# The output projection of block 2 by one level of Strassen's algorithm, its sums made from the merged tiles and the weights

## The chip, the cores and the metric

The kernel is one program on one core of a Trainium2 chip. The metric is the device time of one execution in microseconds (us); lower is better. TensorE is called PE, its weight loads PEld, VectorE DVE, ScalarE ACT, GpSimd POOL, and SyncE, which issues the DMAs, SP. Each engine takes its instructions in the order of its own queue; semaphores tie the queues together.

## The reference

Two transformer blocks over 1024 tokens of width 1024, all in float32. The change lies in the second block, at the line with `w_out`:

```
merged = g_a * (o_a @ w_branch_a[l]) + g_b * (o_b @ w_branch_b[l])
x = x + merged @ w_out[l]
h2 = rms_norm(x, norm2[l])
x = x + jnp.square(jax.nn.relu(h2 @ w_up[l])) @ w_down[l]
```

`merged` and `w_out` are 1024 x 1024; `w_up` is 1024 x 4096.

## The kernel before

A float32 product is made of three fast ones: each operand is split into a high part (ACT casts it, `hi`, L109; tiles `fh`, `hh`, `sh`, `wh`) and a low part (raw minus high, `lo`, L112, on DVE or POOL; tiles `fl`, `hl`, `sl`, `wl`), and PE adds high by high, high by low and low by high into one PSUM bank. An operand tile is 128 x 512.

The order of the instructions is made when the kernel is built. An event list (`e.at(dt, ...)`) holds the work of DVE, ACT, POOL and SP for a time `dt` ns after the present point of PE's estimated time; `e.need(tag)` brings forward whatever carries a tag that PE needs now. A `Stream` hands out one step of its list per `gap` ns until a goal that `ahead` sets; `Feed` is such a stream for operands: its steps load, combine (`comb`, a DVE sum, L1492) and split tiles. One `Feed`, `F`, serves the up and the down projection, which use Strassen's algorithm in Winograd's form already (seven products, in the order 1, 6, 7, 4, 2, 5, 3).

The stages around the change:

- `merge` (L1337) makes `merged` transposed, 16 tiles `gl`, from the two branches and splits each of them (ACT `sh`, DVE `sl`).
- `out2` (L1377) is the output projection as a plain product: two column halves, eight row tiles each, eight steps of k by three matmuls in a tile, 384 matmuls. Its weights come through the weight queue `W` under the names `wp`, split by ACT and POOL.
- `out2_evac` (L1402) follows a tile: the gather (DVE, L1407) adds half of the bank to the residual tile `x`; ACT squares it and sums the row (L407); for the second column half POOL makes 1 over the root mean square (`ry`: L1411, L117, L118) and DVE scales the row, two instructions `xs` (L1415); then the row is stored.
- `prep0` (L1606) turns the first four row tiles into eight operands for the up projection: for each of eight steps, k0 to k7, PE transposes four 128 x 128 pieces (L104) into a PSUM bank `tp` (two of them), ACT makes `hh` and `hr` (L1615, L1616), DVE makes `hl` (L1617). It is interleaved with the matmuls of the second column half. `prep1` does the rows 4 to 7 during `up_first`, the first seven products of the up projection, which follow.

## Time and profile before

| what | us |
|---|---|
| median of 3 runs | 1839.72 |
| lowest and highest | 1838.95, 1840.46 |
| the profiled execution, its own time | 1840.45 |
| its span, first to last instruction | 1838.6 |
| PE busy | 1801.7 (98%) |
| DVE, ACT, POOL busy | 1087.1, 949.3, 702.2 |

A busy PE is one that has matmuls in flight. The projection takes the span from 1107.85 us, its first matmul, to 1199.62 us, the first matmul of the up projection.

### The profile page before, as it was taken

What the parts mean: (1) busy time and instruction counts of PE and PEld (TensorE: products, weight loads), DVE (VectorE), ACT (ScalarE), POOL (GpSimd) and SP (SyncE); (2) the same over time, 40 slices, a digit from 0 to 9 for tenths busy, and PEclk for the clock granted to TensorE, in tenths of its full rate; (3) what the DMA queues carried; (4) which work ended last, traced back from release to release, by engine and by line L of the source; (5) the groups of instructions that cost most, each with busy time, mean ns of one, the idle gap of its engine ahead of it and who ended that gap; (6) DMA issues with size and microseconds to landing.
All of it is one profiled execution on the core that took longest, in us unless ns stands there. A gap on an engine that the chain in (4) does not pass through costs nothing.

```text
span 1838.6 us, 25740 instructions
## 1 busy us (share of the span) xinstructions
PE 1801.7 (98%) x9005; PEld 1517.9 (83%) x9005; DVE 1087.1 (59%) x2033; ACT 949.3 (52%) x1955; POOL 702.2 (38%) x684
## 2 busy tenths in 40 slices
PE   7999999999999999999999999999999998999998
PEld 6888878888898898889888888877888876888886
DVE  6578794544464656556565541467443448766775
ACT  6455553446665767556465322365555555352444
POOL 4123242512222212222111242265544456685873
PEclk9999999999999999999999999999999999999999
DMA  7101131314222221220111922514554478444522
GB/s 204 35 24 35 35 115 59 126 47 93 81 46 81 72 50 47 72 72 27 52 44 48 301 84 83 161 41 156 171 169 146 150 254 290 142 161 138 173 79 92
DMA packets 189186, 195.68 MB, mean 106 GB/s; under 512 B 16944, under 2 KB 124160, under 8 KB 189056
## 3 DMA queue, kind: packets, MB, share of 16 engines
q1 hardware_dynamic: 189056, 194.04, 33.7%
q8 instruction: 70, 1.15, 0.2%
q14 instruction: 60, 0.49, 0.1%
HBM read 141.52 MB, written 54.04 MB: 106 GB/s over the span
## 4 chain that ended last, share of the span: by engine, by line
PE 90%; DVE 3%; ACT 3%; POOL 1%; issue 1%; DMA 1%; SPq 0%; POOLq 0%; ACTq 0%; DVEq 0%
PE mm L99 40%; PE mmO L99 14%; PE mmmm L99 9%; PE mmo L99 7%; PE mmT L99 7%; PE tp L104 4%; PE S L99 4%; PE O L99 4%; DVE s L933 1%; POOL ry L118 0%; DMA wr<-in_w_up 0%; POOL fl L112 0%; DMA x<-x_d 0%; ACT junk L407 0%; PE tp L99 0%
## 5 line engine op out<-in xcount | busy, mean ns | idle before, releaser
L112 POOL TENSOR_TENSOR wl<-wr,wh 128x512 fp32r<-128x512 f32 x164 | 218.9, 1340 | 619.7 <-ACT wh L109 374.4
L99 PE MATMUL mm<-hh,wh 128*128 128x512 f32 (+1 forms) x792 | 313.4, 396 | 0.0
L99 PE MATMUL mm<-hl,wh 128*128 128x512 f32 (+1 forms) x792 | 309.7, 391 | 1.7 <-DVE hl L818 1.7
L99 PE MATMUL mm<-hh,wl 128*128 128x512 f32 (+1 forms) x792 | 309.0, 390 | 0.0
L112 POOL TENSOR_TENSOR fl<-wr,fh 128x512 fp32r<-128x512 f32 x148 | 205.6, 1402 | 129.2 <-ACT fh L109 118.3
L109 ACT CAST fh<-wr 128x512 fp32r<-128x512 f32 x192 | 115.9, 617 | 181.9 <-DVE wr L1492 135.8
L659 ACT ACTIVATE sb<-sb,nm 128x128 f32<-128x128 f32 (+2 forms) x192 | 125.6, 655 | 149.3 <-DVE nm L653 99.1
L99 PEld LDWEIGHTS mm<-hh,wl 128*128 128x128 f32 x792 | 149.4, 189 | 32.4
L99 PEld LDWEIGHTS mm<-hl,wh 128*128 128x128 f32 x792 | 149.8, 189 | 26.6 <-DVE hl L818 2.2
L99 PEld LDWEIGHTS mm<-hh,wh 128*128 128x128 f32 x792 | 149.8, 189 | 25.3
L112 DVE TENSOR_TENSOR ptl<-tp,pth 128x512 fp32r<-128x512 f32 (+2 forms) x176 | 113.4, 646 | 80.2 <-ACT pth L109 76.1
L112 POOL TENSOR_TENSOR fl<-ha,fh 128x512 fp32r<-128x512 f32 x80 | 124.5, 1574 | 47.8 <-ACT fh L109 36.3
L109 ACT CAST pth<-tp 128x512 fp32r<-128x512 f32 (+2 forms) x176 | 96.4, 548 | 74.3 <-PE tp L104 70.1
L668 DVE TENSOR_SCALAR sb<-sb,rc 128x128 f32<-128x128 f32 (+2 forms) x192 | 97.6, 508 | 6.7
L104 PE MATMUL tp<-ident,sb 128*128 128x128 f32 x648 | 99.6, 272 | 1.0 <-DVE ptl L112 0.7
L109 ACT CAST wh<-wr 128x512 fp32r<-128x512 f32 x164 | 99.2, 616 | 0.8 <-DMA wr<-in_w_in 0.4
L104 PEld LDWEIGHTS tp<-ident,sb 128*128 128x128 f32 x648 | 80.6, 140 | 22.4 <-DVE ptl L112 1.2
L99 PE MATMUL O<-pth,v 128*128 128x256 f32 (+3 forms) x264 | 93.2, 361 | 0.0
L99 PE MATMUL mmO<-hh,fh 128*128 128x512 f32 x208 | 81.6, 392 | 2.1 <-ACT pk L1758 2.1
L1492 DVE TENSOR_TENSOR wr<-wr 128x512 f32<-128x512 f32 x96 | 81.4, 848 | 3.7 <-POOL fl L112 2.4
L99 PE MATMUL S<-kh,q 128*128 128x256 f32 (+3 forms) x264 | 79.7, 315 | 2.8 <-DVE nm L653 2.8
L99 PE MATMUL mmO<-hh,fl 128*128 128x512 f32 x208 | 81.6, 393 | 0.0
(296 smaller groups left out, 4529.4 us busy)
## 6 DMA issues: line engine op xcount, KB each, us to landing
wr<-in_w_in SPq DMA_DIRECT2D x116, 256.0 KB, 3.4
ha<-hid_d SPq DMA_DIRECT2D x112, 256.0 KB, 4.2
wr<-in_w_up SPq DMA_DIRECT2D x64, 256.0 KB, 4.6
hid_d<-hc SPq DMA_DIRECT2D x64, 256.0 KB, 2.8
wr<-in_w_down SPq DMA_DIRECT2D x64, 256.0 KB, 3.8
hid_d<-pk SPq DMA_DIRECT2D x45, 256.0 KB, 3.3
wr<-in_w_out SPq DMA_DIRECT2D x32, 256.0 KB, 4.0
x_d<-x SPq DMA_DIRECT2D x32, 256.0 KB, 2.1
```

What stands on the lines that cost most here:

```text
L99: self.nc.tensor.matmul(out=out, lhsT=lhsT, rhs=rhs, start=start, stop=stop, skip_group_check=skip)
L104: self.nc.tensor.transpose(out, in_, ident)
L109: self.nc.scalar.copy(out, in_)
L112: (eng or self.nc.vector).tensor_tensor(out=out, in0=in0, in1=hi.bitcast(F32), op=ALU.subtract)
L659: ACT.activation(d[:, 0:w], d[:, 0:w], AF.Exp, bias=nm, scale=-1.0, accum_out=g.sm[:, j:j + 1])
L668: V.tensor_scalar(out=d[:, 0:w], in0=d[:, 0:w], scalar1=g.rc[:, j:j + 1], scalar2=None, op0=ALU.mult)
L933: V.tensor_tensor(out=nxt[:, a0:1040], in0=cur[:, a0:1040], in1=cur[:, a0 - n:1040 - n], op=ALU.add)
L1492: eng.tensor_tensor(out=self.raw[dst], in0=self.raw[x], in1=self.raw[y], op=op)
```

## The change

The projection becomes seven Strassen products of four 128 x 512 tiles each, with four steps of k by three matmuls: 336 matmuls. `merge` no longer splits its tiles. For q = 0 to 3 `m_sums` makes four sums of merged tiles on DVE as they become complete. A second `Feed`, `FO`, loads the 16 tiles of `w_out`, makes four combinations of them for each q (16 in all, on DVE, now L838), and splits 28 operands of each side: 56 casts on ACT, and 56 low parts, 20 of them on DVE and 36 on POOL. A product's tile is gathered on DVE (now L1554) each time its bank holds a finished sum of the products so far, 28 times; products 4, 2, 5 and 3 finish a quarter of the output, and the gather there is followed by ACT's square; 5 and 3 finish the second column half, so POOL's `ry` (L1563, L117, L118) and DVE's `xs` (L1567) follow theirs. `e.wide` gives the products three pairs of PSUM banks in turn except in products 5 and 3, when the transposes of `prep0` need a pair. The rows 6 and 7 are scaled only after `prep0` has freed the buffers. `row_steps` and `row_prod` are the functions that the down projection had, made common.

```diff
-    for ch in range(2):
-        for j in range(4):
-            W.add(f"wp{ch}{j}", [rowhalf(a["w_out_2"][0], kt, ch) for kt in (2 * j, 2 * j + 1)])
...
+    def row_steps(F, qs, more=None):
+        if more is not None:
+            for i in ORDER:
+                for q in qs:
+                    fn, *keys = more(q, i)
+                    F.source(fn, *keys)
+        def sp(q, n, i, last=True):
+            F.split((q, "a", i), (q, "a", i), True, 5)
+            F.split((q, "w", n), (q, "w", i), last, 5)
+        def cm(q, d, x, y):
+            F.comb((q, "w", d), (q, "w", x), (q, "w", y), SUB)
+        for q in qs:
+            sp(q, "11", 1, False)
+        for q in qs:
+            cm(q, "t3", "12", "22"), cm(q, "12", "12", "11"), cm(q, "11", "22", "12"), sp(q, "11", 6, False)
+        for q in qs:
+            sp(q, "t3", 7)
+        for q in qs:
+            cm(q, "11", "21", "11"), sp(q, "11", 4)
+        for i, n in ((2, "21"), (5, "12"), (3, "22")):
+            for q in qs:
+                sp(q, n, i)
+    def row_prod(F, i, qs, ahead, gather):
+        for q in qs:
+            F.s.need((q, "w", i), ahead)
+        F.flush()
+        ops = [(F.parts.pop((q, "a", i)), F.parts.pop((q, "w", i))) for q in qs]
+        go_on = i in (6, 7, 4, 3)
+        for t in range(4):
+            tc_ = slice(t * 128, t * 128 + 128)
+            if go_on:
+                e.need(("bank", t))
+            else:
+                banks[t] = e.mmt()
+            ps = banks[t]
+            for j, ((h, l), (wh, wl)) in enumerate(ops):
+                e.mm(ps, h[:, tc_], wh, j == 0 and not go_on, False, go_on)
+                e.mm(ps, h[:, tc_], wl, False, False, go_on)
+                e.mm(ps, l[:, tc_], wh, False, j == len(ops) - 1, go_on)
+                yield 650.0
+            e.at(50, lambda t=t, ps=ps: gather(i, t, ps), ("bank", t))
...
+                self.ready(src)
...
+    FO = Feed()
+    FO.look = 8
+    def wo2(q, n, j, ch):
+        r = e.u(name="wr")
+        SY.dma_start(out=r, in_=a["w_out_2"][0][(4 * j + q) * 128:(4 * j + q + 1) * 128, ch * 512:ch * 512 + 512])
+        FO.raw[q, "w", n] = r
+    MORE = {1: (("11", 0, 0),), 6: (("12", 0, 1), ("22", 1, 1)), 4: (("21", 1, 0),)}
+    def out_more(q, i):
+        ws = MORE.get(i, ())
+        return (lambda: [wo2(q, *x) for x in ws], *((q, "w", x[0]) for x in ws))
+    row_steps(FO, range(4), out_more)
+    FO.ready = lambda key: e.need(("ms", key[0])) if key[1] == "a" and key[2] > 1 else None
+    def m_sums(q):
+        m11, m12, m21, m22 = mT.pop((q, 1)), mT.pop((q + 4, 1)), mT.pop((q, 0)), mT.pop((q + 4, 0))
+        s2, s3, s4 = (e.u(name="ms") for _ in range(3))
+        V.tensor_tensor(out=s3, in0=m21, in1=m11, op=SUB)
+        V.tensor_tensor(out=m21, in0=m21, in1=m22, op=ADD)
+        V.tensor_tensor(out=s2, in0=m22, in1=s3, op=ADD)
+        V.tensor_tensor(out=s4, in0=m12, in1=s2, op=SUB)
+        for i, x in {2: m12, 3: s4, 4: m22, 5: m21, 6: s2, 7: s3}.items():
+            FO.raw[q, "a", i] = x
...
-            parts = W.get(f"ab{j}", 1 if j < 5 else 4)
+            parts = W.get(f"ab{j}", 1)
+            if j == 5:
+                for q in range(4):
+                    FO.raw[q, "a", 1] = mT[q, 1]
+                FO.load(0, 8)
+            if j > 5:
+                FO.ahead(8 * (j - 5))
...
-                mT[j, half] = split(ga, ("m", j, half), 1600.0)
+                mT[j, half] = ga
+            if j >= 4:
+                e.at(1800, lambda q=j - 4: m_sums(q), ("ms", j - 4))
...
+    held, rows_free = [], []
...
+    def out2():
+        for n, i in enumerate(ORDER):
+            if n < 4:
+                for t in range(4):
+                    x2_load(i, t)
+            if n >= 4:
+                F.load(0, n - 3)
+                F.ahead(6 * (n - 4))
+            e.wide = i not in (5, 3)
+            yield from row_prod(FO, i, range(4), 16, out2_gather)
...
+    def where(i, t):
+        return t + 4 * (GOES[i][0] == "1"), int(GOES[i][1]) - 1
+
+    def out2_gather(i, t, ps):
+        t, ch = where(i, t)
         xt = x2[t, ch]
+        V.scalar_tensor_tensor(out=xt, in0=ps, scalar=0.5, in1=xt, op0=ALU.mult, op1=ALU.add)
+        if i not in (4, 2, 5, 3):
+            return
...
-        e.at(800, lambda: sumsq(xt, ss[:, ch:ch + 1]))
+        e.at(750, lambda: sumsq(xt, ss[:, ch:ch + 1]))
...
+            if t < 6 or rows_free:
+                e.at(1650, f3, ("xs2", t))
+            else:
+                held.append((f3, ("xs2", t)))
+            xs2_t[t] = e.t + 4450
...
+        rows_free.append(True)
+        for n, (f, tag) in enumerate(held):
+            e.at(50 + 700 * n, f, tag)
...
-    run(out2(0))
-    interleave(out2(1), prep0, lambda: xs2_t.get(3), 2)
-    mT.clear()
+    interleave(out2(), prep0, lambda: xs2_t.get(3), 2)
```

Three places of the queues, with line numbers of the changed kernel where it is that.

DVE in product 1 and on into product 6 (`x2` is a residual tile in a gather, `wr` and `cb` are weight tiles and their combinations; the combination that `fh_11621` and `fl_11622`, the last operand of product 6, are split from is the last row):

```order
L1554 SCALAR_TENSOR_TENSOR x2_11516<-mmT_11565,x2_11516 128x512
L838 TENSOR_TENSOR wr_11239<-wr_11239,wr_11227 128x512
L838 TENSOR_TENSOR wr_11227<-wr_11241,wr_11239 128x512
L838 TENSOR_TENSOR cb_11613<-wr_11243,wr_11245 128x512
L112 TENSOR_TENSOR fl_11610<-wr_11227,fh_11609 128x512
L838 TENSOR_TENSOR wr_11243<-wr_11243,wr_11229 128x512
L838 TENSOR_TENSOR wr_11229<-wr_11245,wr_11243 128x512
```

The gather of product 1's third tile stands ahead of five combinations and one low part. Before, DVE had no weight sums here.

DVE where the rows are scaled. Before, in the second column half:

```order
L1407 SCALAR_TENSOR_TENSOR x2_11862<-mm_11950,x2_11862 128x512
L1415 TENSOR_SCALAR xs_12028<-x2_11587,ry_12025 128x512
L1415 TENSOR_SCALAR xs_12028<-x2_11862,ry_12025 128x512
L1407 SCALAR_TENSOR_TENSOR x2_11901<-mmo_11997,x2_11901 128x512
L1492 TENSOR_TENSOR cb_12073<-wr_11946,wr_11948 128x512
L1617 SCALAR_TENSOR_TENSOR hl_12064<-tp_12057,gains_81,hh_12063 128x512
L1415 TENSOR_SCALAR xs_12092<-x2_11618,ry_12089 128x512
L1415 TENSOR_SCALAR xs_12092<-x2_11901,ry_12089 128x512
L1492 TENSOR_TENSOR wr_11946<-wr_11946,wr_11942 128x512
L1617 SCALAR_TENSOR_TENSOR hl_12097<-tp_12083,gains_81,hh_12096 128x512
```

After, in products 5 and 3, from the gather of the third tile of product 5 (`mmo_12109`); `fl_12142` and `fl_12176` are low parts of the last two weights of product 3, and the gather from `mmo_12031` that stands second to last is that of product 3's first tile:

```order
L1554 SCALAR_TENSOR_TENSOR x2_11715<-mmo_12109,x2_11715 128x512
L112 TENSOR_TENSOR fl_12142<-wr_11241,fh_12141 128x512
L1567 TENSOR_SCALAR xs_12169<-x2_11801,ry_12166 128x512
L1567 TENSOR_SCALAR xs_12169<-x2_11715,ry_12166 128x512
L112 TENSOR_TENSOR fl_12176<-wr_11245,fh_12175 128x512
L838 TENSOR_TENSOR wr_11910<-wr_11916,wr_11914 128x512
L1554 SCALAR_TENSOR_TENSOR x2_11717<-mm_12146,x2_11717 128x512
L838 TENSOR_TENSOR wr_11912<-wr_11912,wr_11910 128x512
L1567 TENSOR_SCALAR xs_12200<-x2_11803,ry_12197 128x512
L1567 TENSOR_SCALAR xs_12200<-x2_11717,ry_12197 128x512
L1554 SCALAR_TENSOR_TENSOR x2_11598<-mmo_12031,x2_11598 128x512
L1567 TENSOR_SCALAR xs_12227<-x2_11512,ry_12224 128x512
```

Two low parts that PE needs in product 3 now stand between the scalings of product 5's rows, and each further gather behind the scaling of the row before.

DVE a little later, where the operands of `prep0` begin (`hl_12250` is the one of step k0, `hl_12277` that of k1):

```order
L1554 SCALAR_TENSOR_TENSOR x2_11600<-mm_12070,x2_11600 128x512
L838 TENSOR_TENSOR wr_12018<-wr_12018,wr_12014 128x512
L1567 TENSOR_SCALAR xs_12263<-x2_11514,ry_12260 128x512
L1567 TENSOR_SCALAR xs_12263<-x2_11600,ry_12260 128x512
L1679 SCALAR_TENSOR_TENSOR hl_12250<-tp_12240,gains_81,hh_12249 128x512
L838 TENSOR_TENSOR wr_12014<-wr_12020,wr_12018 128x512
L1554 SCALAR_TENSOR_TENSOR x2_11602<-mmo_12109,x2_11602 128x512
L1679 SCALAR_TENSOR_TENSOR hl_12277<-tp_12269,gains_81,hh_12276 128x512
L1679 SCALAR_TENSOR_TENSOR hl_12299<-tp_12288,gains_81,hh_12298 128x512
```

The low part of k0 stands behind the scalings of the rows 4 and 5, which come from product 3's first two tiles.

PE at the end of the projection. Before (buffer numbers left out), the last transposes, those of k7, are followed by six more matmuls of their tile and by the 24 matmuls of the last tile:

```order
L104 MATMUL tp<-ident,xs 128x128 x4
L99 MATMUL mmo<-wh,sh 128x512
L99 MATMUL mmo<-wl,sh 128x512
L99 MATMUL mmo<-wh,sl 128x512
L99 MATMUL mmo<-wh,sh 128x512
L99 MATMUL mmo<-wl,sh 128x512
L99 MATMUL mmo<-wh,sl 128x512
L104 MATMUL tp<-ident,xs 128x128 x4
L99 MATMUL mmo<-wh,sh 128x512
L99 MATMUL mmo<-wl,sh 128x512
L99 MATMUL mmo<-wh,sl 128x512
L99 MATMUL mmo<-wh,sh 128x512
```

After, in the last tile of product 3: the transposes of k2 stand just ahead of the first row, those of k3 are the second group, and the four groups of k4 to k7 are one row, x16, with no matmul between them, right ahead of the up projection:

```order
L99 MATMUL mm<-fh 128x512
L99 MATMUL mm<-fl,fh 128x512
L99 MATMUL mm<-fh,fl 128x512
L99 MATMUL mm<-fh 128x512
L99 MATMUL mm<-fl,fh 128x512
L99 MATMUL mm<-fh,fl 128x512
L104 MATMUL tp<-ident,xs 128x128 x4
L99 MATMUL mm<-fh 128x512
L99 MATMUL mm<-fl,fh 128x512
L99 MATMUL mm<-fh,fl 128x512
L104 MATMUL tp<-ident,xs 128x128 x16
L99 MATMUL mmo<-hh,fh 128x512
```

The transposes begin later in the projection, and half of them have moved behind its last matmul.

## Rows read from the trace of the kernel before

**Rows 1.** The page of the profile: the span, the busy time of the engines, and the shares of the engines in the chain of work that ended last.

```profile
span 1838.6 us, 25740 instructions
...
PE 1801.7 (98%) x9005; PEld 1517.9 (83%) x9005; DVE 1087.1 (59%) x2033; ACT 949.3 (52%) x1955; POOL 702.2 (38%) x684
...
PE 90%; DVE 3%; ACT 3%; POOL 1%; issue 1%; DMA 1%; SPq 0%; POOLq 0%; ACTq 0%; DVEq 0%
```

**Rows 2.** Busy time by stretch: the end of the merge, the projection, and the start of the up projection. Columns: the stretch in us from the start of the span and its length; busy us and (x) number of instructions of PE, PEld, DVE, ACT and POOL; the granted clock of TensorE as a share of 2.4 GHz; the busy share of the DMA engines and GB/s.

```profile
1060.00:1108.00 48.00, 48.00 (x213) 39.75 (x212) 23.75 (x35) 13.41 (x24) 19.53 (x15) 1.00 0.37 119
1108.00:1200.00 92.00, 91.46 (x419) 75.25 (x418) 31.91 (x49) 28.05 (x60) 24.16 (x34) 1.00 0.33 107
1200.00:1250.00 50.00, 47.13 (x225) 39.01 (x224) 30.19 (x37) 31.77 (x58) 37.83 (x30) 1.00 0.09 27
```

**Rows 3.** The timeline of PE at the two ends of the projection: its first matmul, one near its end, its last one, and the first of the up projection. Columns: start us, busy us, engine, line, operation, tiles.

```profile
1107.85 0.39 PE L99 MATMUL mmo<-wh,sh 128*128 128x512 f32 x1
...
1197.12 0.39 PE L99 MATMUL mm<-wl,sh 128*128 128x512 f32 x1
...
1199.39 0.39 PE L99 MATMUL mm<-wh,sl 128*128 128x512 f32 x1
1199.62 0.39 PE L99 MATMUL mmo<-hh,fh 128*128 128x512 f32 x1
```

**Rows 4.** Groups of instructions by line between 1108 and 1200 us (the projection and the transposes in it). Columns: line, engine, operation, tiles, shapes, count | busy us in all, mean ns of one | idle us of the engine just before them, and what ended it.

```profile
L1415 DVE TENSOR_SCALAR xs<-x,ry 128x512 f32<-128x512 f32 x14 | 9.2, 700 | 12.3 <-POOL ry L118 12.3
...
L1617 DVE SCALAR_TENSOR_TENSOR hl<-tp,gains,hh 128x512 fp32r<-128x512 f32 x8 | 6.0, 747 | 1.1 <-ACT hr L1616 1.1
...
L1615 ACT ACTIVATE hh<-tp,gains 128x512 fp32r<-128x512 f32 x8 | 5.5, 690 | 3.8 <-PE tp L104 3.8
...
L104 PE MATMUL tp<-ident,xs 128*128 128x128 f32 x32 | 4.9, 276 | 0.5 <-DVE hl L1617 0.5
...
L1492 DVE TENSOR_TENSOR wr<-wr 128x512 f32<-128x512 f32 x6 | 4.1, 683 | 0.0
```

**Rows 5.** The timeline of DVE, ACT and POOL after one tile of the second column half of the projection, from the gather to the scaled rows, and, later, ACT's two calls on one bank of `prep0` and the scaling after another tile. In brackets: the idle time before, and what ended it; a row with x2 holds two instructions.

```profile
1173.33 0.69 DVE L1407 SCALAR_TENSOR_TENSOR x<-mm,x 128x512 f32<-128x512 f32 x1 [0.81 <-PE mm L99]
...
1174.12 0.60 ACT L407 ACTIVATE junk<-x 128x512 f32<-128x512 f32 x1 [4.21 <-DVE x L1407]
...
1174.92 0.20 POOL L1411 TENSOR_TENSOR ss<-ss 128x1 f32<-128x1 f32 x1 [3.07 <-ACT junk L407]
...
1175.47 0.55 POOL L118 TENSOR_TENSOR ry<-ry,mhalf 128x1 f32<-128x1 f32 x1
...
1175.99 1.29 POOL L112 TENSOR_TENSOR fl<-wr,fh 128x512 fp32r<-128x512 f32 x1
1176.06 1.90 DVE L1415 TENSOR_SCALAR xs<-x,ry 128x512 f32<-128x512 f32 x2 [2.04 <-POOL ry L118]
...
1187.04 0.69 ACT L1615 ACTIVATE hh<-tp,gains 128x512 fp32r<-128x512 f32 x1
...
1187.63 0.68 ACT L1616 ACTIVATE hr<-tp,gains 128x512 f32<-128x512 f32 x1
...
1190.69 0.88 DVE L1415 TENSOR_SCALAR xs<-x,ry 128x512 f32<-128x512 f32 x2 [1.00 <-POOL ry L118]
```

**Rows 6.** Groups of instructions by line between 1200 and 1300 us, where the up projection runs and POOL is busier, with the columns of rows 4.

```profile
L112 POOL TENSOR_TENSOR fl<-wr,fh 128x512 fp32r<-128x512 f32 x28 | 39.5, 1424 | 13.9 <-ACT fh L109 13.4 <-DMA hid_d<-u 0.4
...
L109 ACT CAST fh<-wr 128x512 fp32r<-128x512 f32 x28 | 16.8, 616 | 12.3 <-DVE wr L1492 6.8 <-POOL hl L112 3.8 <-POOL fl L112 1.7
...
L1492 DVE TENSOR_TENSOR wr<-wr 128x512 f32<-128x512 f32 x11 | 9.7, 884 | 2.6 <-POOL fl L112 2.4
...
L1492 DVE TENSOR_TENSOR cb<-wr 128x512 f32<-128x512 f32 x4 | 4.6, 1140 | 0.0
```

**Rows 7.** The timeline at two places where POOL and DVE each run an operation on tiles that lie in SBUF.

```profile
1267.41 1.29 POOL L112 TENSOR_TENSOR fl<-wr,fh 128x512 fp32r<-128x512 f32 x1 [1.53 <-ACT fh L109]
...
1267.55 1.70 DVE L1689 TENSOR_TENSOR pk<-u,hc 128x512 f32<-128x512 f32 x1
...
1269.11 1.27 POOL L112 TENSOR_TENSOR fl<-wr,fh 128x512 fp32r<-128x512 f32 x1 [0.41 <-ACT fh L109]
1269.36 1.57 DVE L1691 TENSOR_TENSOR hc<-pk 128x512 f32<-128x512 f32 x1
```

**Rows 8.** PE after a wait of 2.14 us: four matmuls from its timeline, the last of them near the end of the slow stretch; then busy time by stretch, there and in and after a wait that ends at 1224.8 us, with the columns of rows 2.

```profile
1271.27 0.50 PE L99 MATMUL mmO<-hh,fh 128*128 128x512 f32 x1 [2.14 <-ACT pk L1758]
...
1272.38 0.63 PE L99 MATMUL mmO<-hh,fh 128*128 128x512 f32 x1
1272.81 0.63 PE L99 MATMUL mmO<-hl,fh 128*128 128x512 f32 x1
...
1275.49 0.40 PE L99 MATMUL mmO<-hh,fl 128*128 128x512 f32 x1
...
1270.00:1274.00 4.00, 2.73 (x7) 2.22 (x8) 3.64 (x5) 3.00 (x6) 2.84 (x3) 0.71 1.04 393
...
1221.00:1225.00 4.00, 1.13 (x6) 0.63 (x5) 3.81 (x5) 3.97 (x9) 4.00 (x4) 1.00 0.00 0
1225.00:1230.00 5.00, 5.00 (x23) 4.12 (x24) 4.60 (x5) 4.74 (x10) 5.00 (x4) 1.00 0.00 0
```

**Rows 9.** The waits of PE between 1108 and 1250 us: instruction, what it waited for, us in total, times, longest.

```profile
PE mm L99 <- DVE hl L1635: 2.9, 1, 2.9
```

## What the change does to the time: the prediction

> **What bounds the kernel now.** The page comes first: PE has matmuls in flight in 98% of the span, and 90% of the chain that ended last is PE's [rows 1]. So a matmul taken away is worth its time, as long as PE's next operands are there. Second, the busy time by stretch: from 1108 to 1200 us, the projection, PE is busy 91.46 of 92 us at full clock, with DVE at 31.91, ACT at 28.05 and POOL at 24.16 [rows 2]. Third, PE's waits: in the projection only 0.5 us, behind the low parts of `prep0`, and then 2.9 us behind DVE's low parts (L1635) at the start of the up projection [rows 9]. Nothing but PE sets the projection's length now. Its other engines have room on average; whether they have it at the right moment is the question here, since the change gives them shorter deadlines.
>
> **The saving.** Ten matmuls follow one another in 1199.39 - 1197.12 = 2.27 us, 0.227 us each [rows 3]. The products have 336 matmuls instead of 384: 48 x 0.227 = 10.9 us less. A product lasts 48 x 0.227 = 10.9 us and one of its tiles 2.72 us, where a tile of before lasted 24 x 0.227 = 5.45 us. Before, first matmul to first matmul of the up projection is 1199.62 - 1107.85 = 91.8 us [rows 3]. I count from that first matmul as zero and ask when the up projection can begin after the change.
>
> **The split of `merged`** left ACT and DVE in the merge, where PE waits for nothing and DVE is busy 23.75 of 48 us [rows 2]; the sums of the merged tiles, four per q, take the place of the low parts there. I cost both at nothing; PE hides them. Two matmuls' time either way is the bound, since product 1's operands are split before the merge ends.
>
> **Product 6, first tile.** Its last operand comes through DVE, ACT and POOL in a row. The gather of product 1's third tile can start when that tile is done, 8.3 us (three tiles and the drain of the last matmul, 0.39 - 0.23 us), and takes 0.69 [rows 5]. Behind it stand five weight sums and a low part, each 0.68 where POOL is quiet [rows 4], then the cast, 0.62, and POOL's low part, 1.3 to 1.42 [rows 5, 6]: 8.3 + 0.7 + 6 x 0.68 + 0.62 + 1.3 = 15.0 us. PE wants it as its eleventh matmul of the product, at 10.9 + 2.3 = 13.2 us. That is a wait of 1.8 us at least. But POOL is making low parts all the while. Where both engines read SBUF, the rows show them taking turns: DVE 1.70 and 1.57 us for sums that began just behind a low part of POOL [rows 7], and sums of this kind at 0.884 and 1.140 us on average where POOL is busy, against 0.683 [rows 4, 6]. I take 1.06 each, which gives 8.3 + 0.7 + 6.4 + 0.62 + 1.42 = 17.4: a wait of 4.2 us. If each of the six were held as in rows 7, it would be about 6.
>
> The page "SBUF — State Buffer" of the Trainium skill, in "Who interferes with whom", has a harder rule than this mean: a DVE instruction with two SBUF inputs and a GpSimd instruction that reads SBUF share a port pair as an exclusive lock, and the loser blocks for the whole instruction. By that rule with a POOL operation in front of each of the six, the wait would be the 6 us, by the quiet rows 1.8; rows 7 agree with the lock, rows 6 say that not every sum meets one.
>
> **Product 4** has the same chain with two sums and a low part behind the gather of product 7's third tile. Product 7 starts at 2 x 10.9 + 4.2 = 26.0, so its operand is there at 26.0 + 8.3 + 0.7 + 3 x 0.68 + 0.62 + 1.3 = 39.0 at best, 40.2 at the higher prices, and up to 40.7 if the low part just ahead of it on POOL is late too; PE wants it at 26.0 + 10.9 + 2.3 = 39.2. A wait of 0 to 1.5 us, taken as 1.2. Products 7, 2 and 5 have their operands early: none of their last low parts stands behind a gather of the product just before that could end later than it. Product 5 thus starts at 5 x 10.9 + 4.2 + 1.2 = 59.9.
>
> **Products 5 and 3: the scaling of the rows.** This is the place that decides. After a gather, ACT squares, POOL makes `ry`, and only then DVE scales: from the start of a gather to the start of `xs` it was 1176.06 - 1173.33 = 2.73 us, of which DVE idled 2.04 waiting for `ry`; the two `xs` then took 1.90 us beside a low part of POOL, and 0.88 without one [rows 5]. So a row costs DVE 3.6 to 4.6 us in its queue. Before, a tile came every 5.45 us and this fitted. Now one comes every 2.72, and since the next gather stands behind the `xs` of the row before, DVE falls behind by 0.9 to 1.9 us a tile, and whatever stands between them waits too. By the order: the first gather of product 5 at 59.9 + 2.72 + 0.16 = 62.8; `xs` from 65.5 to 67.4; a low part (0.7); second gather at 68.1, `xs` from 70.9 to 72.8; a sum (0.7); third gather at 73.5, `xs` from 76.2 to 78.1; then `fl_12176`, done at 78.8. Product 3 was to start at 70.8 and wants that at 73.1. **PE waits about 5.7 us** in product 3's first tile. A low part of POOL stands beside each of these three scalings, so I took 1.90.
>
> It goes on: a sum, fourth gather at 79.5, `xs` from 82.2 to 83.1 (no low part beside it); gather of product 3's first tile, 83.1, `xs` from 85.8 to 87.7 (one beside it); a sum; the next gather at 88.4, `xs` from 91.1 to 92.0; and only now the low part of k0, 0.75 [rows 4], done at 92.8. PE, meanwhile, has done tiles one to three and the transposes of k0 and k1 (32 transposes of before were 4.9 us of busy time, 0.61 us a step with the drain of the last [rows 4]; I take 0.45 without it) by about 86.5, and stands before those of k2, which need the bank that k0's low part reads. **A second wait of about 6 us**, to 92.8. Then k2, six matmuls, k3 (whose bank is free at 94.9, after a sum, a gather and another low part), three matmuls: the projection's last ends at 96.1.
>
> **The tail.** k4 to k7 now have no matmul between them; each waits for the bank of two steps before. ACT's `hh` and `hr` follow one another in 0.59 us [rows 5] (0.69 for one alone [rows 4]), the squares of product 3's last tiles stand among them, and DVE's `hl` closes each bank: `hl` of k2 at 97.0, k3 98.2, k4 100.7, k5 103.2, and the transposes of k7 end at 103.6. The up projection can start there, 7.5 us after the projection's last matmul; pure PE time in it is 1.8 us. Before, all eight steps lay among matmuls, with 0.5 us of waits [rows 9].
>
> **The up projection.** `prep1` comes 24 matmuls after its start rather than 30. The wait of 2.9 us at its start [rows 9] may shrink by as much, since POOL got on during PE's waits, or grow by as much, with POOL at 4.00 of 4 us there [rows 8]; I take zero.
>
> **The sum.** 103.6 - 91.8 = +11.8 us: -10.9 of matmuls, +4.2 and +1.2 in products 6 and 4, +5.7 and +6 in product 3, +5.7 of the tail that is not the transposes' own time. Against the profiled execution's 1840.45 this is 1852.3; the median lies 0.7 lower, so **1852 us**. At the low end of each price (product 6 at 1.8, product 4 at 0, every pair of `xs` at 0.88): product 5 starts at 56.3, k0's low part is done at 59.2 + 6 x 3.61 + 3.5 + 0.75 = 85.1, the up projection starts at 95.9, +4.1: 1844. At the high end (6 and 1.5, every pair at 1.90, each sum and low part between them at 1.3): about +22, 1862. So if this mechanism holds, 1844 to 1862.
>
> **Rivals.** (a) *The queues keep pace after all, and it is faster.* It hangs on one period: from gather to gather in product 5. At 2.72 us or less there is no wait in product 3, and the transposes flow: 336 x 0.227 + 4 x 0.45 + 1.8 + 7.5 gives a start at 87.4, -4.4 us: 1835; with the tail hidden too, 81.8 and 1830. For it: DVE, ACT and POOL are each at a third of the stretch [rows 2]. Against it: 2.73 us are latency that no load explains [rows 5]. (b) *The waits are real but the low prices hold and something is given back.* At +4.1, less the 2.9 us of L1635, it is +1.2: 1841, no change. (c) *The clock falls.* After 2.14 us of waiting the granted clock was 0.71 in the next stretch, and matmuls came 0.43 us apart, the pace of 1.2 GHz, until about 1275 [rows 8]: some ten matmuls, 2 us. After the 2.9 us before 1224.8 it stayed at 1.00 [rows 8]. With waits of 4, 6, 6 and the tail, up to four such falls add 2 to 8 us: 1854 to 1860, and beyond with high prices.
>
> For (c) the Trainium skill, "TensorE: Matmul & The Clock Gate", Part 1, says that an array that idles is put to 1.2 GHz and comes back once it is busy; by it each long wait here would cost those 2 us. The first place of rows 8 agrees, the second does not.
>
> **How the numbers follow.** My mechanism without a fall of the clock 0.50, with it 0.18, (b) 0.13, (a) 0.19. Within 0.2%, about 3.7 us, a measurement can't tell this kernel from no change. Faster is (a), 0.19; same is (b), 0.13; slower 0.68. The likeliest case gives 1852, its own range 1844 to 1862. To leave out no more than 2 in 10 the range must take in (b) and the near half of (a): 1834 to 1862.
>
> **What would show it.** In the profile after: `ry` named as what ends DVE's idle time before L1567, some 2 us each, and gathers of product 5 about 4 to 5 us apart; PE waiting for a POOL low part 13 us after the merge, for a DVE low part (L112) and then for L1679 in product 3; four groups of transposes with gaps of over 1 us at the end. I am wrong if gathers there stand 2.7 us apart, or if PE waits in product 3 for none of these.

## The result, and the profile after

The changed kernel takes 1863.17 us (median of 4 runs, 1861.86 to 1863.99) against 1839.34 beside it: the ratio is 1.0129, 95% interval 1.0111 to 1.0146. It is 23.8 us slower. Slower was forecast, by 12; the time lies 1.2 us above the range. The page of the profile, with the lines that answer to [rows 1]:

```profile
span 1861.5 us, 25745 instructions
...
PE 1802.8 (97%) x8957; PEld 1513.3 (81%) x8957; DVE 1132.7 (61%) x2081; ACT 962.3 (52%) x1979; POOL 733.7 (39%) x704
...
PE 86%; DVE 6%; issue 3%; ACT 3%; POOL 2%; DMA 1%; POOLq 0%; SPq 0%; ACTq 0%; DVEq 0%
```

PE is busy as long as before, although it has 48 matmuls fewer; the span grew by 22.9 us, and PE's share of the chain fell from 90% to 86%. Busy time by stretch, the columns of [rows 2]; the up projection now starts at 1219.62 us:

```profile
1060.00:1108.00 48.00, 48.00 (x213) 39.77 (x212) 33.81 (x45) 7.06 (x12) 13.10 (x9) 1.00 0.23 78
1108.00:1200.00 92.00, 80.35 (x315) 62.27 (x314) 56.93 (x73) 35.81 (x76) 47.09 (x47) 0.89 0.29 93
1200.00:1222.00 22.00, 12.53 (x60) 9.33 (x59) 12.19 (x20) 11.74 (x22) 4.42 (x11) 0.85 0.19 71
```

The merge is as it was, PE without a gap. The projection has PE at 80.35 of 92 us and at a granted clock of 0.89, and it reaches into the next stretch, where PE is busy 12.53 of 22 us. DVE went from 31.91 to 56.93 us and POOL from 24.16 to 47.09. PE's five largest waits between 1108 and 1260 us, in the form of [rows 9]:

```profile
PE tp L104 <- DVE hl L1679: 9.5, 5, 3.4
PE mmo L99 <- DVE fl L112: 6.4, 3, 3.6
PE mmo L99 <- POOL fl L112: 3.5, 1, 3.5
PE mmmm L99 <- ACT fh L109: 2.5, 1, 2.5
PE mm L99 <- POOL fl L112: 2.0, 1, 2.0
```

The transposes' banks (9.5 us), low parts of DVE (6.4) and a cast (2.5) are most of what PE waits for in the projection, with 2.7 us in smaller waits for casts and for POOL's low parts; the 3.5 and 2.0 for POOL come in the up projection.

From the first matmul of the projection, at 1107.56 us, to the first of the up projection it is 1219.62 - 1107.56 = 112.1 us, where before it was 91.8; from there to the end 641.9 us against 639.0. So 20.3 us were lost in the projection and 2.9 behind it. The places, read from PE's, DVE's and POOL's timelines:

| us after the first matmul | predicted | measured |
|---|---|---|
| product 6's last operand there | 17.4 | 17.2 |
| product 7 starts | 26.0 | 28.5 |
| product 5 starts | 59.9 | 62.4 |
| first scaling starts | 65.5 | 71.2 |
| `fl_12176` done (product 3's first tile) | 78.8 | 86.1 |
| k0's low part done | 92.8 | 99.5 |
| last matmul starts | 95.9 | 102.4 |
| up projection starts | 103.6 | 112.1 |

PE in product 6 (start, busy us):

```profile
1120.59 0.40 PE L99 MATMUL mmmm<-fh,fl 128*128 128x512 f32 x1
1123.45 0.80 PE L99 MATMUL mmmm<-fh 128*128 128x512 f32 x1 [2.46 <-ACT fh L109]
1124.80 0.80 PE L99 MATMUL mmmm<-fl,fh 128*128 128x512 f32 x1 [0.56 <-POOL fl L112]
...
1125.82 0.63 PE L99 MATMUL mmO<-fh 128*128 128x512 f32 x1
...
1130.62 0.40 PE L99 MATMUL mmT<-fh 128*128 128x512 f32 x1
```

The tenth matmul waits for the cast, the eleventh for POOL's low part, as worked out, until 17.2 us. But from 1125.82, the second tile's first matmul, to 1130.62, the third's, twelve matmuls take 4.80 us, where such twelve take 2.72 elsewhere. The granted clock from 1124.0 to 1130.3 us is 0.51, the lower of its two levels, 1.2 GHz.

DVE and POOL from product 5's first gather on, then the low part that product 3's first tile lacks, and k0's:

```profile
1173.23 0.69 DVE L1554 SCALAR_TENSOR_TENSOR x<-mmo,x 128x512 f32<-128x512 f32 x1 [1.15 <-PE mmo L99]
...
1173.84 3.81 POOL L112 TENSOR_TENSOR fl<-wr,fh 128x512 fp32r<-128x512 f32 x3
...
1178.16 0.55 POOL L118 TENSOR_TENSOR ry<-ry,mhalf 128x1 f32<-128x1 f32 x1
...
1178.68 4.15 POOL L112 TENSOR_TENSOR fl<-wr,fh 128x512 fp32r<-128x512 f32 x3
1178.75 2.94 DVE L1567 TENSOR_SCALAR xs<-x,ry 128x512 f32<-128x512 f32 x2 [4.83 <-POOL ry L118]
...
1181.61 1.76 DVE L112 TENSOR_TENSOR fl<-ms,fh 128x512 fp32r<-128x512 f32 x1
...
1183.30 0.68 DVE L1554 SCALAR_TENSOR_TENSOR x<-mm,x 128x512 f32<-128x512 f32 x1
...
1192.93 0.68 DVE L112 TENSOR_TENSOR fl<-wr,fh 128x512 fp32r<-128x512 f32 x1
...
1206.32 0.75 DVE L1679 SCALAR_TENSOR_TENSOR hl<-tp,gains,hh 128x512 fp32r<-128x512 f32 x1
```

The chain is the one that was drawn: gather, `ry`, two `xs`, a low part, the next gather. Its first round is far longer than in [rows 5]: three low parts of POOL stand ahead of `ry`, so the scaling starts 5.5 us after the gather and not 2.73; with two more low parts beside it the pair takes 2.94 us, and DVE's own low part behind it, beside POOL's next one, 1.76. The second gather starts at 1183.30, 10.1 us after the first. PE in product 3 and in the tail:

```profile
1185.35 0.80 PE L99 MATMUL mmo<-fh 128*128 128x512 f32 x1 [1.42 <-ACT fh L109]
1189.75 0.80 PE L99 MATMUL mmo<-fl,fh 128*128 128x512 f32 x1 [3.60 <-DVE fl L112]
...
1193.67 0.80 PE L99 MATMUL mmo<-fl,fh 128*128 128x512 f32 x1 [1.88 <-DVE fl L112]
...
1207.12 0.66 PE L104 MATMUL tp<-ident,xs 128*128 128x128 f32 x4 [3.42 <-DVE hl L1679]
...
1210.00 0.40 PE L99 MATMUL mm<-fh,fl 128*128 128x512 f32 x1
...
1215.54 1.11 PE L104 MATMUL tp<-ident,xs 128*128 128x128 f32 x4 [2.20 <-DVE hl L1679]
1218.86 1.12 PE L104 MATMUL tp<-ident,xs 128*128 128x128 f32 x4 [2.20 <-DVE hl L1679]
1219.62 0.78 PE L99 MATMUL mmo<-hh,fh 128*128 128x512 f32 x1
```

PE waits 3.60 and 1.88 us for low parts of DVE, 3.42 us for k0's bank (the end of that wait is 99.6 us after the first matmul), and 2.20 us each ahead of k6 and k7, whose transposes run at 1.11 us instead of [rows 4]'s 0.6. The granted clock is 0.50 from 1190 to 1198 us, in product 3, and 0.50 from 1216 to 1219.6 us, in the tail; from 1207 to 1212 us, behind the wait of 3.42 us, it is 1.00.

### The profile page after: what moved, and what is told of

Its sections match the earlier page's. It is cut to its first block, busy times and chain, and to the rows that moved or that the text cites. A ratio compares the mean times of both kernels' runs of the same rounds, so it can differ in the third digit from the quotient of the medians.

```text
span 1861.5 us, 25745 instructions
## 1 busy us (share of the span) xinstructions
PE 1802.8 (97%) x8957; PEld 1513.3 (81%) x8957; DVE 1132.7 (61%) x2081; ACT 962.3 (52%) x1979; POOL 733.7 (39%) x704
## 4 chain that ended last, share of the span: by engine, by line
PE 86%; DVE 6%; issue 3%; ACT 3%; POOL 2%; DMA 1%; POOLq 0%; SPq 0%; ACTq 0%; DVEq 0%
PE mm L99 37%; PE mmmm L99 14%; PE mmT L99 9%; PE mmO L99 7%; PE mmo L99 5%; PE tp L104 4%; PE S L99 4%; PE O L99 4%; POOL fl L112 1%; DVE wr L838 1%; DVE s L1055 1%; ACT junk L404 1%; POOL ry L118 0%; DMA ha<-hid_d 0%; DVE sb L665 0%
## 5 line engine op out<-in xcount | busy, mean ns | idle before, releaser
L112 POOL TENSOR_TENSOR wl<-wr,wh 128x512 fp32r<-128x512 f32 x148 | 198.5, 1347 | 561.7 <-ACT wh L109 320.5
L112 POOL TENSOR_TENSOR fl<-wr,fh 128x512 fp32r<-128x512 f32 x161 | 228.7, 1434 | 146.4 <-ACT fh L109 122.1
L109 ACT CAST fh<-wr 128x512 fp32r<-128x512 f32 x216 | 130.4, 617 | 222.0 <-DVE wr L838 170.1
L109 ACT CAST wh<-wr 128x512 fp32r<-128x512 f32 x148 | 89.9, 617 | 20.7 <-DMA wr<-in_w_branch_a 16.1
L104 PEld LDWEIGHTS tp<-ident,sb 128*128 128x128 f32 x648 | 80.5, 140 | 22.9 <-DVE ptl L112 1.8
L838 DVE TENSOR_TENSOR wr<-wr 128x512 f32<-128x512 f32 x108 | 95.0, 880 | 1.6
L99 PE MATMUL mmmm<-fh 128*128 128x512 f32 x212 | 83.4, 393 | 6.7 <-ACT fh L109 6.7
L99 PE MATMUL mmmm<-fl,fh 128*128 128x512 f32 x212 | 83.8, 395 | 2.4 <-POOL fl L112 1.8
L99 PE MATMUL mmmm<-fh,fl 128*128 128x512 f32 x212 | 83.0, 391 | 0.0
```

The costliest lines, as they stand in the source:

```text
L99: self.nc.tensor.matmul(out=out, lhsT=lhsT, rhs=rhs, start=start, stop=stop, skip_group_check=skip)
L104: self.nc.tensor.transpose(out, in_, ident)
L109: self.nc.scalar.copy(out, in_)
L112: (eng or self.nc.vector).tensor_tensor(out=out, in0=in0, in1=hi.bitcast(F32), op=ALU.subtract)
L838: eng.tensor_tensor(out=self.raw[dst], in0=self.raw[x], in1=self.raw[y], op=op)
```

## The experiments

e1 to e5 and e8 have the changed kernel as their base, e6 has e5, and e7, e9, e10 and e12 have e6. The theory: PE loses its time at five separate places (product 6's operand, DVE's queue behind the scalings, the transposes' banks, the work for the up projection, POOL's first rounds of it), and each can be taken out by an edit of its own. The rivals are in the expectations. For each kernel, from its profile: when the up projection starts, and how long the rest of the span is.

| kernel | median us | up projection starts | rest of the span |
|---|---|---|---|
| before | 1839.3 | 91.8 | 639.0 |
| changed | 1863.2 | 112.1 | 641.9 |
| e1 no up feed | 1857.3 | 102.2 | 646.1 |
| e2 late scaling | 1858.5 | 105.5 | 644.0 |
| e3 more banks | 1856.5 | 105.4 | 640.6 |
| e4 early sums | 1854.5 | 102.0 | 643.4 |
| e8 busy wait | 1862.8 | 110.2 | 643.5 |
| e5 = e2 + e3 + e4 | 1843.4 | 90.8 | 645.0 |
| e6 = e5, further ahead | 1843.5 | 89.6 | 642.8 |
| e7 = e6, no up feed | 1844.5 | 88.0 | 647.3 |
| e9 = e6, half by ACT | 1842.6 | 89.8 | 644.0 |
| e10 = e6, up feed sooner | 1839.4 | 91.4 | 638.3 |
| e12 = e6 and four edits | 1835.2 | 88.8 | 638.2 |

The last two columns are of one profiled execution each, and its time can lie off the median: by 2.3 us in e6, whose profiled execution was the fastest of its ten. Product 6, whose code is the same in the changed kernel, e1, e2 and e3, loses 0.9 us less in e1 and e3 than in the other two. So a difference of 1 us between two kernels in these columns is not yet an effect of the edit.

**e1: the up projection's operands out of products 5 and 3.**

```diff
-            if n >= 4:
-                F.load(0, n - 3)
-                F.ahead(6 * (n - 4))
```

> Base: the changed kernel (1863.2 us). One edit: the steps of the up projection's operands (loads, sums, splits) no longer run inside products 5 and 3; they come when the up projection asks for them. Theory A (the waits of product 3 come mostly from the latency of the row scaling, which stands in DVE's queue): the first scaling's ry comes about 2.4 us sooner, for want of POOL low parts ahead of it, the sums and the locks between the scalings go, about 4 us, so the up projection can start some 5 to 8 us sooner than its 112.1 us after the merge, and most of that is paid back as PE waits at the start of the up projection: 1858 to 1866 us. Rival B (the added work for the up projection is itself the cause of the loss): product 3 runs without waits, the up projection starts at 95 us or sooner and the time falls below 1850 us.

1857.26 us, 0.7 below theory A's range. DVE in the first round of product 5, without the up projection's low parts on POOL:

```profile
1171.69 0.69 DVE L1551 SCALAR_TENSOR_TENSOR x<-mmo,x 128x512 f32<-128x512 f32 x1 [1.14 <-PE mmo L99]
...
1174.71 1.91 DVE L1564 TENSOR_SCALAR xs<-x,ry 128x512 f32<-128x512 f32 x2 [2.33 <-POOL ry L118]
...
1177.14 0.68 DVE L1551 SCALAR_TENSOR_TENSOR x<-mm,x 128x512 f32<-128x512 f32 x1
```

The scaling starts 3.0 us after the gather instead of 5.5, the pair takes 1.91 us instead of 2.94, the low part behind it 0.68 instead of 1.76, and the second gather comes 5.45 us after the first instead of 10.1. The up projection starts 9.9 us sooner, 0.9 of it from product 6, which this edit does not touch; that is more than the 5 to 8 expected, and the rest of the span grows by 4.2. Neither theory in full: the added low parts and sums weigh more than I held, but without them product 3 still waits 2.2 us for DVE, and the transposes 2.1 for k0's bank.

**e2: DVE scales a row behind the next tile's gather.** POOL's part of `f3` stays; the two scalings go into a function `f5` of their own.

```diff
+            e.at(1650, f3)
...
-                e.at(1650, f3, ("xs2", t))
+                e.at(3400, f5, ("xs2", t))
...
-            xs2_t[t] = e.t + 4450
+            xs2_t[t] = e.t + 3400 + 2800
```

> Base: the changed kernel (1863.2 us). One edit: POOL makes ry when it did, but DVE's two scalings of a row are put into the queue 3.4 us after the gather instead of 1.65 us, that is behind the next tile's gather; the transposes begin 0.1 us later by plan, and five groups instead of four fall behind the last matmul. Theory A (DVE idles for ry, 12.6 us in all between 1173 and 1207 us, while PE's operands stand behind it): those idle times shrink to under 4 us, the waits of PE in product 3's first tile fall from 7.8 to under 3 us, the wait of k2 falls too, and the time is 1850 to 1857 us. Rival C (DVE and POOL have simply too much to do there, whatever the order): DVE's idle time goes, but the up projection starts within 3 us of where it did, 1860 to 1864 us.

1858.53 us: 4.6 faster, 1.5 above theory A's range. The group of scalings in the changed kernel, and then in e2, with the idle time ahead of them last:

```profile
L1567 DVE TENSOR_SCALAR xs<-x,ry 128x512 f32<-128x512 f32 x15 | 11.7, 819 | 13.3 <-POOL ry L118 12.6 <-PE tp L104 0.6
```

```profile
L1570 DVE TENSOR_SCALAR xs<-x,ry 128x512 f32<-128x512 f32 x14 | 10.2, 770 | 3.7 <-POOL ry L118 3.1 <-PE tp L104 0.6
```

DVE's idle time for `ry` went from 12.6 to 3.1 us as expected. PE's waits in product 3's first tile fell from 7.8 us to one of 4.5, for a low part of DVE, and not under 3: POOL is busy 14.49 of the 15 us from 1173 to 1188 there, and the first pair of scalings takes 2.93 us still. The last matmul of the projection starts 9.5 us sooner, at 92.9; but five groups of transposes stand behind it now, the tail, counted from that start, is 12.6 us long instead of 9.6, and the up projection starts 6.6 us sooner. So rival C, which allowed 3, falls; what is left of it is a busy POOL.

**e3: banks of the products for k6 and k7.**

```diff
+            elif k == 6:
+                ps = tr4(0, k, e.mmp.tile([128, 512], F32, name="mm", tag="mm"))
+            else:
+                ps = tr4(0, k, e.op.tile([128, 512], F32, name="mmo", tag="O"))
```

> Base: the changed kernel (1863.2 us). One edit: the transposes of k6 and k7 go into a bank of the pools mm and O, free since product 3's gathers, instead of waiting for the two banks tp. Theory A (the tail is a round of PE, ACT and DVE over two banks): the two waits of 2.2 us before k6 and k7 go, the up projection starts about 5 us sooner, and the time is 1857 to 1860 us. Rival D (the tail is hidden, since the up projection's first operands wait on POOL anyway, 3.5 and 2.0 us): the waits at 1242 and 1254 us grow by as much and the time stays within 1.5 us of 1863.

1856.52 us. PE at the end of the tail, from k5 on:

```profile
1211.31 0.63 PE L104 MATMUL tp<-ident,xs 128*128 128x128 f32 x4 [0.69 <-DVE hl L1684]
1211.78 0.60 PE L104 MATMUL mm<-ident,xs 128*128 128x128 f32 x4
1212.21 0.60 PE L104 MATMUL mmo<-ident,xs 128*128 128x128 f32 x4
1212.57 0.48 PE L99 MATMUL mmo<-hh,fh 128*128 128x512 f32 x1
```

k5 to k7 follow one another and the up projection starts 0.36 us behind k7's first transpose: 6.7 us sooner, of which 0.9 comes in product 6, that this edit does not touch. The tail is 4.0 us long instead of 9.6, and nothing of that is paid back (the rest of the span even is 1.3 us shorter). The time is 0.5 us below theory A's range. Rival D falls: the tail was on the path.

**e4: the sums of `w_out` earlier.**

```diff
+    FO.s.gap = 1000.0
...
-                FO.ahead(8 * (j - 5))
+                FO.ahead(11 * (j - 5))
...
-            yield from row_prod(FO, i, range(4), 16, out2_gather)
+            yield from row_prod(FO, i, range(4), 20, out2_gather)
```

> Base: the changed kernel (1863.2 us). One edit: the steps of w_out (sums and splits) are spread earlier and closer: one in 1.0 us instead of 1.5, with goals of 11 and 22 steps instead of 8 and 16 by the last two steps of the merge, and 20 ahead instead of 16, so that the six operations before the last operand of product 6 no longer stand in a row. Theory A: PE's wait of 3.7 us in product 6's first tile goes, and with it the half-speed matmuls behind it (2.7 us), the 1.2 us of product 4 may go too: product 5 starts at 55 to 57 us after the merge instead of 62.4, and the time is 1856 to 1859 us. Rival E (what is won in product 6 is lost again in product 3, where DVE and POOL set the pace): the chain of gathers and scalings starts sooner by as much, so a rival would show product 3's waits grown by 5 us and the time within 2 us of 1863.

1854.53 us, the largest gain of a single edit, 1.5 below theory A's range. PE's tenth and eleventh matmul of product 6:

```profile
1120.87 0.51 PE L99 MATMUL mmmm<-fh 128*128 128x512 f32 x1 [0.34 <-ACT fh L109]
1122.22 0.50 PE L99 MATMUL mmmm<-fl,fh 128*128 128x512 f32 x1 [0.84 <-POOL fl L112]
```

The waits there are 0.34 and 0.84 us, product 7 starts at 23.5 us instead of 28.5 and product 5 at 56.2 instead of 62.4. Product 3's waits, 7.8 us in its first tile, become one of 6.0 for a low part of DVE, where rival E had them grow by 5 us. Its second tile starts 10.6 us sooner and the up projection 10.0: rival E falls.

**e8: matmuls that nobody reads, in the place of the wait.** 16 of them in product 6's first tile, into a spare bank.

> Base: the changed kernel (1863.2 us). One edit: 16 matmuls whose result nobody reads stand in the place where PE waits in product 6's first tile (11 ahead of its tenth matmul, 5 ahead of the eleventh), on operands that are there, into a bank that is free: PE is busy in that wait, and the wait itself does not end sooner. Theory C (the fall of the granted clock after the wait costs time of its own): the tenth and eleventh matmuls start when they did, 15.9 and 17.2 us after the merge, but product 6's second tile takes 2.7 us instead of 4.8 and product 7 starts at 26 us instead of 28.5: 1860 to 1861.5 us. Rival (the clock's fall is made up later, in waits that come anyway): product 7 starts at 26 us, but the time stays at 1863 within 1 us. Rival (the clock falls all the same): product 7 starts at 28.5.

PE in e8, the added matmuls to the bank S, and at the end the wait for k0's bank:

```profile
1120.57 2.67 PE L892 MATMUL S<-fh 128*128 128x512 f32 x11
1123.21 0.50 PE L99 MATMUL mmmm<-fh 128*128 128x512 f32 x1
1123.55 1.31 PE L896 MATMUL S<-fh 128*128 128x512 f32 x5
...
1125.17 0.40 PE L99 MATMUL mmO<-fh 128*128 128x512 f32 x1
...
1127.90 0.39 PE L99 MATMUL mmT<-fh 128*128 128x512 f32 x1
...
1204.28 0.66 PE L104 MATMUL tp<-ident,xs 128*128 128x128 f32 x4 [3.71 <-DVE hl L1688]
...
1206.54 0.63 PE L99 MATMUL mm<-fh,fl 128*128 128x512 f32 x1
```

The waits end when they did (the tenth matmul at 1123.21, 15.9 us after the first), the granted clock is 1.00 from 1123.3 to 1130.0 us, the second tile takes 1127.90 - 1125.17 = 2.73 us, and product 7 starts at 26.0 us instead of 28.5: the fall of the clock cost 2.5 us at this place. The lead is kept through products 5 and 3, where DVE's chain starts sooner by as much: product 5 starts at 59.9 us instead of 62.4, the last tile of product 3 at 92.4 instead of 95.3.

It is lost behind that. After the wait for k0's bank, 3.71 us here, matmuls soon come 0.43 us apart (granted clock 0.65 from 1204 to 1208 us), where the changed kernel kept full clock after 3.42 us at the same place, and the last matmul starts only 1.1 us sooner. The up projection starts 1.9 us sooner, and its thirteenth matmul 0.9, since eleven matmuls there come at half the clock and not six. The time is 1862.77: no difference that can be told. The second rival's numbers came. Of its reason the first half is seen, a loss made up later; but it was falls of the clock at other places, and not waits, that took the lead, and why they lay otherwise is not shown.

The page "TensorE: Matmul & The Clock Gate" of the Trainium skill, Part 1, says that the clock follows how busy the array has been; at this place these runs agree, 0.51 after the empty wait and 1.00 after the filled one.

**e5: e2, e3 and e4 together.**

> Base: the changed kernel (1863.2 us). The edits of e2 (late scaling), e3 (other banks for k6 and k7) and e4 (sums earlier) together. Theory A (the waits are separate places, each paid once, so their gains add): e4 took 10.0 us from the start of the up projection, e2 6.6, e3 6.7 by the traces; the last two share the tail (e2 leaves five groups there), so 18 to 21 together: the up projection starts 91 to 94 us after the merge, the time is 1842 to 1846 us. Rival E (one engine's total work sets the pace in products 5 and 3, so the gains overlap): the up projection starts at 97 us or later, 1848 us or more.

1843.40 us, ratio 1.0018 (1.0008 to 1.0027); the up projection starts at 90.8 us. Theory A. Single gains were 4.6, 6.7 and 8.6, in sum 19.9; together 19.8.

**e6: the steps of `w_out` still further ahead.**

```diff
-    FO.s.gap = 1000.0
+    FO.s.gap = 900.0
...
-            yield from row_prod(FO, i, range(4), 20, out2_gather)
+            yield from row_prod(FO, i, range(4), 20 if n < 3 else 40, out2_gather)
```

> Base: e5_all. One more edit: the steps of w_out run one in 0.9 us and up to 40 steps ahead from product 4 on, so that product 3's low parts are in DVE's and POOL's queues ahead of the scalings rather than between them. Theory A: the wait for DVE's low part in product 3's first tile (6.0 us in e4, 4.5 in e2) falls under 2 us, the up projection starts 3 to 5 us sooner than in e5_all, the time is 1837 to 1842 us, about that of the kernel before. Rival E (total work): the same wait shows elsewhere in products 5 and 3, and the time is that of e5_all within 1.5 us.

1843.52 us, as e5. The wait in product 3's first tile is 2.4 us in both. Rival E, for this wait: moving the low parts further ahead no longer helps.

**e7: e6 without the up projection's operands in products 5 and 3.**

> Base: e6_far. One more edit: no steps of the up projection's operands inside products 5 and 3, as in e1. In e1 this started the up projection 9.9 us sooner and cost 4 us of it there, a gain of 6. Theory A: with the scalings off the critical way the gain in product 3 is small (0 to 3 us) and the cost in the up projection the same 4 us, so this is 1 to 4 us slower than e6_far. Rival B (the work for the up projection is the load that counts there): it is 2 us or more faster than e6_far.

1844.51 us, 1.0 slower than e6, just theory A. Product 3 runs with no wait in its tiles, but PE's waits at the start of the up projection are now these:

```profile
PE mmo L99 <- ACT fh L109: 2.4, 2, 1.4
PE mm L99 <- ACT fh L109: 2.3, 1, 2.3
PE mmo L99 <- POOL fl L112: 2.1, 3, 0.9
PE mm L99 <- DVE hl L1707: 1.9, 1, 1.9
```

Work for the up projection that isn't done in the projection is paid for behind it: the rest of the span is 4.5 us longer by the two profiles, and by the medians, with a start 1.6 us sooner, some 2.6.

**e9: ACT scales the first half of a row.**

```diff
-                for j in range(2):
-                    V.tensor_scalar(out=xs[:, 512 * j:512 * j + 512], in0=x2[t, j], scalar1=rs[t], scalar2=None, op0=ALU.mult)
+                ACT.activation(xs[:, 0:512], x2[t, 0], AF.Copy, scale=rs[t])
+                V.tensor_scalar(out=xs[:, 512:1024], in0=x2[t, 1], scalar1=rs[t], scalar2=None, op0=ALU.mult)
```

> Base: e6_far (1843.5 us). One edit: the first half of each row is scaled by ACT, which is idle for 6 us on end in product 5, the second half by DVE as before. Theory A (DVE's queue is what PE still waits for in product 3, 2.4 us, and DVE is busy without a gap there): that wait falls under 1 us, the up projection starts 2 to 4 us sooner than 89.6 us after the merge, and the time is 1840 to 1842.5 us. Rival (the up projection takes it back, as it took back 4 to 8 us in e1 and e7): the up projection starts sooner, but the time stays within 1 us of 1843.5.

1842.61 us, 0.9 less than e6: not to be told from it. The wait falls from 2.4 to 1.8 us only, and not under 1. The last matmul starts 2.2 us sooner, but the up projection does not: the tail is 8.6 us long instead of 6.2, and the granted clock in it is 0.56 (1190.5 to 1197.0 us), where e6's is 1.00 (1191.0 to 1196.6).

**e10: the up projection's operands one product sooner.**

```diff
-            if n >= 4:
-                F.load(0, n - 3)
-                F.ahead(6 * (n - 4))
+            if n >= 3:
+                F.load(0, min(N0, n - 2))
+            if n >= 4:
+                F.ahead(6 * min(N0, n - 3))
```

> Base: e6_far (1843.5 us). One edit: the operands of the up projection are begun one product sooner (6, 12, 18 steps in products 2, 5, 3 instead of 0, 6, 12), which is the 18 steps that the kernel before had done by the same point. Theory A (what e5 to e7 gained in the projection was paid back at the start of the up projection, whose low parts were not made: waits for POOL and ACT there of 6.1 us in e6_far, against 2.9 in the kernel before): these waits fall by 3 us or more, the waits in product 3 grow by less than 2, and the time is 1839.5 to 1842 us. Rival E (POOL and DVE are full in products 5 and 3): the start of the up projection moves later by as much as its waits shrink, 1843 to 1845 us.

1839.41 us, ratio to the kernel before 1.0001 (0.9992 to 1.0010), 4.1 less than e6 (3.7 with each held against the kernel before beside it) and 0.1 below theory A's range. Two of PE's waits:

```profile
PE mm L99 <- DVE hl L1711: 2.9, 1, 2.9
PE mmo L99 <- DVE fl L112: 2.8, 1, 2.8
```

The waits for POOL and ACT at the start of the up projection are gone, what is left there is the 2.9 us behind `hl` that the kernel before had [rows 9]; the projection itself is 1.8 us longer. Theory A.

**e12: e10 and e9, the transposes 1.3 us sooner by plan, and other banks for k4 and k6.**

```diff
...
-            xs2_t[t] = e.t + 3400 + 2800
+            xs2_t[t] = e.t + 3400 + 1500
...
```

> Base: e6_far (1843.5 us). Four edits: those of e9 and e10; the transposes begin 1.3 us sooner by plan, so that four groups and not five fall behind the last matmul; and of these k4 and k6 take banks of the pools mm and O, k5 and k7 the two banks tp. Theory A (each of these places still costs what the trace of e6_far shows): the wait of 2.4 us in product 3, about 4 of the 6 us between the last matmul and the up projection, and 3 us of its first waits go: 1833 to 1838 us, faster than the kernel before. Rival E (total work of DVE and POOL): 1840 to 1844 us.

1835.17 us (11 runs), ratio 0.9978, interval 0.9969 to 0.9987: 4 us faster than the kernel before. Its largest waits of PE from 1108 to 1260 us:

```profile
PE tp L104 <- DVE hl L1690: 2.3, 3, 1.8
PE mmo L99 <- DVE fl L112: 2.3, 1, 2.3
PE mm L99 <- POOL fl L112: 1.3, 1, 1.3
```

The projection takes 88.8 us and the rest 638.2. Which of the four edits gave how much over e10 was not tried one by one. Of the 10.9 us of matmuls saved, 4 are now kept; among what still takes the rest are 2.3 us of waiting in product 3's first tile and 2.3 us for the transposes' banks.

## Why the prediction was right and wrong

**Right.** The direction, and what PE waits for at every place: the cast and POOL's low part in product 6, product 4's 1.2 us, `ry` as what ends DVE's idle time ahead of the scalings, the low part of DVE that product 3 lacks, the transposes of k2 behind k0's low part, the tail over two banks. From `fl_12176` to k0's low part the chain was worked out as 14.0 us and took 13.5. That the last operand of product 6 came within 0.2 us (17.2 against 17.4) is luck in part: the gather ended at 9.9 us instead of 9.0, behind a low part that took 1.78, and the six operations behind it took 5.3 us instead of 6.4. e3 and e4 each took one of the places out and gained what stood there; e2 gained 9.5 us in products 5 and 3 and gave 3 back in the tail.

**Wrong: the size.** +11.8 us were forecast and 23.8 came. In the order of the steps:

- **Product 6 (term +4.2; measured 6.8).** The wait was right; the fall of the clock behind it was left to a rival at 0.18 instead of standing in the sum. e8 puts it at 2.5 us, and everything up to the last tile of product 3 comes later by that.
- **Products 5 and 3, the first round (term +5.7 for product 3's first tile; its waits measured 7.8, on a start that was already 2.9 us late).** This is the step that failed. I costed every `ry` at the 2.73 us of [rows 5], a row in whose round POOL had nothing else to do, although the change gives POOL low parts of both feeds at this point; three of them stood ahead of `ry`. The first scaling started 5.5 us after its gather, its pair took 2.94 us with two low parts beside it (I had let one lie beside it), the low part behind it 1.76 (I had 0.7): the second gather came 10.1 us after the first instead of 5.3. That is 4.8 us. e1 shows the cause: without the up projection's low parts the same round took 5.45 us. Of the rule that the prediction weighed for two SBUF inputs, the lock in "SBUF — State Buffer" of the Trainium skill ("Who interferes with whom"), the trace agrees in the 1.76 us: that low part began 0.24 us behind one of POOL and ended 0.55 us after it. I had priced no lock there.
- **k0's bank (term +6; measured 3.4).** The low part came 6.7 us later than worked out, but PE, after product 3's first tiles, stood there more than 9 us later. The half clock in product 3's second tile (4.5 us instead of 2.72) went into this wait.
- **The tail (7.5 us; measured 9.4 from the last matmul's end).** k6's and k7's transposes ran at half the clock, and the round over PE, ACT and DVE was 3.3 us per step instead of 2.5.
- **The up projection (term 0; measured +2.9).** The bound of 2.9 us either way held, at its upper end: its low parts were not made (12 steps instead of the 18 of before), and PE waited 3.5 and 2.0 us for POOL. e10 makes those 18 steps and the rest of the span falls to 638.3.

Against the table above, the up projection starts 8.5 us later than worked out: 2.5 by the clock behind product 6, 4.8 by the first round, 2.0 by the tail, less 0.8 between. The 2.9 behind its start come on top.

**The range.** Its upper end, 1862, priced high bounds of product 6 and of the scalings with a quiet POOL ahead of `ry` and without the clock; the time was 1.2 us above. Its own terms do not give that end: with product 5 at 62.0 us, six rounds of 4.63 us and five sums and low parts of 1.3 end k0's low part at 99.9 us, and the up projection starts at 110.7, which is +19 us and not +22. And six operations held as in [rows 7], at 1.6 us each, make product 6 wait about 7.5 us and not 6. That the stated end lay so near the time is luck. Rival (a) fell: it needed a period of 2.72 us in product 5, and the first two gathers were 10.1 us apart. Rival (b) fell with it: nothing was given back behind the start of the up projection. Rival (c) was right about the falls of the clock, and its 2 us for each is near the 2.5 behind product 6; in product 3 the fall was hidden in the next wait.

What stays open: how the 23.8 us divide when several waits overlap. The single edits give 5.9, 4.6, 6.7 and 8.6 us, 25.8 in sum, more than was lost; e8's 2.5 us at its place came to 0.4. Not tried was `ry` ahead of POOL's low parts with the up projection's feed left where it is. When a wait is followed by half clock and when not is open too.

## What to carry to other kernels

When matmuls are taken away, look not at the mean load of the other engines but at the deadline of each operand: the time from the last thing that can start it, through every queue it passes, with what stands ahead of it in those queues. A row from a quiet stretch gives the latency of a chain, and not its price where the same engine has been given twice the work. A chain over three engines belongs behind the next tile's work in the first engine's queue, and the work for the next stage must not be dropped to make room, since it is paid for there.

## What the runs showed of the hardware that I had not expected

Two `xs` of DVE took 0.88 us beside an idle POOL, 1.90 beside one low part [rows 5] and 2.94 beside two. Three times in the projection PE ran at half its clock after its waits, twelve matmuls in 4.80 us, and after the wait of 3.42 us it did not; at that same place in e8 a wait of 3.71 us was followed by half clock. With 16 matmuls in product 6's wait that nobody reads the clock stayed at 1.00 and the next product started 2.5 us sooner, but the kernel's time did not change. The same code of product 6 lost 0.9 us more in two executions (the changed kernel, e2) than in two others (e1, e3).
